# MLA latents and one chunk of the feed-forward input turned on VectorE in a two-layer decoder trunk

## The chip, the core and the metric

The kernel runs on one core of a Trainium2 chip. The metric is the time of one execution on the device, in microseconds (us). Engines are called by the profile's names: PE is TensorE, DVE is VectorE, ACT is ScalarE, POOL is GpSimd, and SP issues the loads. All arithmetic is float32.

## The reference, cut to what matters

```python
for l in range(DEPTH):                      # 2 layers, SEQ 256, D_MODEL 2048
    h = rmsnorm(x, g_mix[l])
    (fq, fk, fv, ff, cq, ckv, kr, uv, dq, dk, dv) = jnp.split(h @ w_in[l], pts, axis=-1)
    ...
    y_b = mla_mixer(cq, ckv, kr, g_cq[l], g_ckv[l], w_uq[l], w_ukv[l], cos_mla, sin_mla)
    ...
    x = x + jnp.concatenate([y_a, y_b, y_c, y_d], axis=-1) @ w_o[l]
    x = x + memory_cross_attention(rmsnorm(x, g_cross[l]), mem_n, ...)
    x = x + swiglu(rmsnorm(x, g_ffn[l]), w_gate[l], w_up[l], w_down[l])
return rmsnorm(x, g_final)

def mla_mixer(c_q, c_kv, k_rope, g_cq, g_ckv, w_uq, w_ukv, cos, sin):
    q = _heads(rmsnorm(c_q, g_cq) @ w_uq, MLA_HEADS)       # c_q: 256 x 384
    kv = _heads(rmsnorm(c_kv, g_ckv) @ w_ukv, MLA_HEADS)   # c_kv: 256 x 256
    ...
def swiglu(xn, w_gate, w_up, w_down):                      # hidden width 5632
    return (jax.nn.silu(xn @ w_gate) * (xn @ w_up)) @ w_down
```

## The kernel before

The 256 rows of x stand on the partitions as two tiles of 128, and the 2048 columns are four chunks of 512 (`self.x[c]`). Every large product is split in two float32r parts on either side: a weight block is copied to `whi` by ACT (line 204) and the rest `wlo = raw - whi` is made by DVE (line 210). Each product then takes three matmuls (lines 303 to 305): left high by `whi`, left high by `wlo`, left low by `whi`. The left operand must stand turned, with the contracted columns on the partitions, so a normalised chunk of x becomes `fT_hi` (ACT, line 206) and `fT_lo` (DVE, line 212) after a transpose. The row factor of the norm is applied later, to the product.

There are two ways to turn. `turn` (line 420) uses PE: 128x128 transposes against the identity into PSUM. `turn_blocks` (line 429) uses DVE: sixteen 32x32-block transposes for a chunk, into an SBUF tile `raw`, four to a step.

`drive` sets the order on all engines; it is written out as a program, and each engine runs its own part of it in order. Work is cut into groups (one product of 512 columns, such as `gate` of one hidden block), and groups into units of two k-tiles, which are 12 matmuls. For unit i the loop first converts the weights of unit i + 3 (`AHEAD` is 3), then issues the matmuls of unit i, then calls `step`, which advances every running task (a Python generator) by one `yield`. So what a task issues is placed between units, and a `yield` is one unit. If a unit needs a chunk whose task has not ended, `need` drains the task there, after the conversion of unit i + 3 and before the matmuls of unit i. `whi` and `wlo` have 5 buffers, so the conversion for unit i + 3 waits until PE is done with unit i - 2. SBUF tiles of one chunk's size come from a ring of 21 slots.

The latents: group `m1` gives cq (384 columns), `m2` gives ckv (256). `latent` squares, scales by the norm, and turns the two or three 128-column blocks on PE (tiles `cqtp`, `ckvtp`). In program order the turning of cq falls behind units 4 and 5 of `m2`, that of ckv behind unit 4 of `dk`; cq is used by `uqr` and `uqn` (after `dk`), ckv by `ukn` after them. Group `dq`, which came first, is being turned by DVE at the same time (tile `dqT`, two transposes a step), and `gates` makes the forget gate's cumulative sums.

The feed-forward input: `wco` (cross attention's output product) has four groups, one for each chunk c of x, of two units each. When group c ends, `into_x` adds it to x (line 950) and starts `norm_chunk`: squares first, and from the third step on, PE transposes (tile `xT`) with the high and low parts. The first `gate` product then takes the chunks in the order 0, 1, 2, 3, two units to a chunk. In two other places of a layer (`wo` into cT, `down` into hT) `norm_chunk` runs with `early`, that is with `turn_blocks`, for the first three chunks.

Of the kernel before, what the change touches and what calls it, by code (L numbers as in the profile page):

```python
# [25 lines left out]
NC = 4  # L26
# [115 lines left out]
class Kernel:  # L142
# [196 lines left out]
        stats = self.const.tile([P, T * NC], F32, name=name + "st")  # L339
        return Split(NC), stats[:].rearrange("p (t c) -> p t c", t=T)  # L340

    def norm_chunk(self, st, c, g, name, early):

        nc, xs, stats, xc = self.nc, st[0], st[1], self.x[c]
        part = xs.parts[c] = self.split_tile(name)
        for t in range(T):
            self.square_sum(xc[:, t, :], stats[:, t, c : c + 1])
        st[4] += 1
        yield
        yield  # L350
        if early:
            raw = self.slot("xT")
            yield from self.turn_blocks(xc[:], raw)
            yield
        for b in range(2):
            tv = raw[:, 2 * b : 2 * b + 2, :] if early else self.turn(xc, 2 * b, 2, "xT")
            self.split_turned(tv, part, 2 * b, self.gains[:, g, 4 * c + 2 * b : 4 * c + 2 * b + 2])
            yield
# [63 lines left out]

    def turn_blocks(self, nat, dst, n=4):

        src = nat.rearrange("p t (c b i) -> p t c b i", c=4, b=4)
        for i in range(16):
            a, b = i % 4, i // 4
            o = dst[32 * b : 32 * b + 32].rearrange("p c (t a j) -> p t c a j", t=T, a=4)
            self.nc.vector.transpose(o[:, :, :, a, :], src[32 * a : 32 * a + 32, :, :, b, :])  # L429
            if i % n == n - 1:  # L430
                yield
# [231 lines left out]
    def latent(self, nat, w, nk, off, l, name, xs):  # L663

        nc = self.nc
        ss = self.sm(name + "ss", T)
        for t in range(T):
            self.square_sum(nat[:, t, :], ss[:, t : t + 1])
        rc = self.rms(ss[:], T, w, name + "r")
        for _ in range(3):  # L670
            yield
        for t in range(T):
            nc.vector.tensor_scalar(nat[:, t, :], nat[:, t, :], rc[:, t : t + 1], None, ALU.mult)
        yield
        yield
        part = xs.parts[0]
        for b in range((nk + 1) // 2):
            n = min(2, nk - 2 * b)
            tv = self.turn(nat, 2 * b, n, name + "tp")
            self.split_turned(tv, part, 2 * b, self.gsm[:, l, off + 2 * b : off + 2 * b + n])  # L680
            yield

    def gates(self, z, rows, own):
# [258 lines left out]
        for c in range(NC):  # L942
            yield Group("wo", self.blocks("w_o", l, c), 512, y, False, self.into_x(c, st, 1 + 3 * l, "cT", c < NC - 1), O_ORDER, begin=mem if c == NC - 1 else None, hold=0 if c else 4)

    def into_x(self, c, st=None, g=None, name=None, early=False):

        def f(ps):
            for t in range(T):
                x = self.x[c][:, t, :]
                self.nc.vector.tensor_tensor(out=x, in0=ps[t][:], in1=x, op=ALU.add)  # L950
            if st is not None:
                st[0].tasks[c] = [self.soon(self.norm_chunk(st, c, g, name, early))]
                if c == NC - 1:
                    self.norm_after(st)
        return f
# [125 lines left out]
    def cross(self, l, norm, st, memT, mres):  # L1081
        s = {}
        y, cT = Split(1), norm[0]

        def out_q(ps):
            nat = self.slot("cq", shape=(P, T, 512))
            self.out_natural(ps, 0, 512, nat, self.times(norm[2][0], 128.0 ** -0.5))
            s["q"] = self.slot("cqT")
            yield
            yield from self.turn_blocks(nat[:], s["q"])  # L1090

        def done_q(ps):
            norm[3].drain()
            s["tq"] = self.soon(out_q(ps))

        def done_k(ps):
            self.mem_rms.drain()
            kT = self.slot("ckT")
            s["tk"] = self.soon(self.out_turned(ps, kT, mres[1]))
            s["p"] = [self.slot("cpT", shape=(P, 2, 512)) for _ in range(2)]  # L1100
            s["heads"] = [self.later(self.attend_memory((s["tq"], s["tk"]), s["q"], kT, h, s["p"][h // 2][:, h % 2, :])) for h in range(4)]

        def out_v(ps, hh):
            if hh == 0:
                s["v"] = self.slot("cv", shape=(P, T, 512))
                y.parts[0] = self.split_tile("yc")
            v = s["v"]
            self.out_natural(ps, 0, 256, v[:, :, 256 * hh : 256 * hh + 256], mres[0])
            yield
            for t in s["heads"][2 * hh : 2 * hh + 2]:  # L1110
                t.drain()
            o = self.bank("co")
            for i in range(2):
                h = 2 * hh + i
                for kt in range(2):
                    self.nc.tensor.matmul(o[:, i * S : (i + 1) * S], v[:, kt, h * P : (h + 1) * P], s["p"][hh][:, i, kt * S : (kt + 1) * S], start=(i == 0 and kt == 0), stop=(i == 1 and kt == 1))
            ov = o[:].rearrange("p (i s) -> p i s", i=2)
            self.split(ov, y.parts[0][0][:, 2 * hh : 2 * hh + 2, :], y.parts[0][1][:, 2 * hh : 2 * hh + 2, :])

        def done_v(hh):  # L1120
            def f(ps):
                s["tv%d" % hh] = self.soon(out_v(ps, hh))
                if hh == 1:
                    y.tasks[0] = [s["tv0"]]
                    y.late = s["tv1"]
            return f

        yield Group("cq", self.blocks("w_cq", l), 512, cT, False, done_q)
        yield Group("ck", self.blocks("w_ck", l), 512, memT, True, done_k)
        for hh in range(2):  # L1130
            yield Group("cv", self.blocks("w_cv", l, hh, 8), 256, memT, False, done_v(hh))
        for c in range(NC):
            yield Group("wco", self.blocks("w_co", l, c), 512, y, False, self.into_x(c, st, 2 + 3 * l, "fT"), hold=0 if c else 1)


    def ffn(self, l, norm, st):
        nc, a, fT = self.nc, self.a, norm[0]
        s = {}

        def done_gate(ps):  # L1140
            norm[3].drain()
            r = norm[2][0]
            s["g"] = self.slot("silu", shape=(P, T, 512))
            for t in range(T):
                nc.scalar.activation(s["g"][:, t, :], ps[t], AF.Silu, bias=0.0, scale=r[:, t : t + 1])

        def out_up(ps, g, part):
            r = norm[2][0]
            for t in range(T):
                nc.vector.scalar_tensor_tensor(out=g[:, t, :], in0=ps[t], scalar=r[:, t : t + 1], in1=g[:, t, :], op0=ALU.mult, op1=ALU.mult)  # L1150
            yield
            raw = self.slot("hidT")
            yield from self.turn_blocks(g, raw)
            for b in range(2):
                self.split(raw[:, 2 * b : 2 * b + 2, :], part[0][:, 2 * b : 2 * b + 2, :], part[1][:, 2 * b : 2 * b + 2, :])
                yield

        def done_up(hid, j):
            def f(ps):
                hid.parts[j] = self.split_tile("hid")  # L1160
                hid.tasks[j] = [self.soon(out_up(ps, s["g"], hid.parts[j]))]
            return f

        for j0, j1 in ((0, 6), (6, NCH)):
            hid = Split(j1 - j0)
            for j in range(j0, j1):
                yield Group("gate", self.blocks("w_gate", l, j), 512, fT, False, done_gate)
                yield Group("up", self.blocks("w_up", l, j), 512, fT, False, done_up(hid, j - j0))
            for c in range(NC):
                w = [(a["w_down"][l, c, b], 4) for b in range(j0, j1)]  # L1170
                if j1 < NCH:
                    done = self.into_x(c)
                elif l + 1 < L:
                    done = self.into_x(c, st, 3 * (l + 1), "hT", c < NC - 1)
                else:
                    done = self.final(c, st[1])
                yield Group("down", w, 512, hid, False, done, last=(l == L - 1 and j1 == NCH and c == NC - 1))
# [170 lines left out]
```

## Time and profile before

| | |
|---|---|
| median of 3 runs | 2336.83 us (2336.59 to 2338.02) |
| the profiled execution | 2337.07 us, of which the trace spans 2335.4 us |
| PE busy | 2322.1 us of the span |
| DVE busy | 1501.7 us |
| ACT busy | 1132.1 us |
| POOL busy | 231.1 us |
| mean granted PE clock | 0.999 of full speed |

Matmuls overlap, so the duration shown for one (390 ns for 512 columns) is longer than the time from one start to the next. What a stretch of PE costs is read from the starts. The times of a row are in us from the start of the span.

### The profile page before, as it was taken

How to read it: one execution, taken by the hardware profiler on the slowest of the kernel's cores; microseconds unless marked ns; L12 is line 12 of the kernel's file. 1: busy time of each engine (PE TensorE's matmuls, PEld its weight loads, DVE VectorE, ACT ScalarE, POOL GpSimd, SP SyncE). 2: the span in 40 equal slices, each digit the busy share in tenths (PEclk: the TensorE clock that was granted, in tenths of full speed). 3: DMA queues.
4: the chain of work that ended last, by engine and by line, in shares of the span. 5: the costliest groups of instructions: out<-in, count | busy, mean ns of one | idle time of the engine just before them, and what ended most of it. 6: DMA issues, size and time to landing. Idle time of an engine off the chain costs nothing.

```text
span 2335.4 us, 28342 instructions
## 1 busy us (share of the span) xinstructions
PE 2322.1 (99%) x10992; PEld 1950.9 (84%) x10992; DVE 1501.7 (64%) x2183; ACT 1132.1 (48%) x1611; POOL 231.1 (10%) x174
## 2 busy tenths in 40 slices
PE   9999999999999999999999999999999999999998
PEld 8888889888888888888898888898888888888886
DVE  6846796566766446767766567955666564476564
ACT  7656554644444344444455565636444433344443
POOL 1221340100000000000012314301000000000001
PEclk9999999999999999999999999999999999999999
DMA  8644565455555555555545454644555555555543
GB/s 295 223 165 164 190 214 183 165 196 181 195 202 198 195 187 188 193 204 186 194 165 193 163 175 166 215 180 162 211 183 186 213 190 191 197 180 199 216 180 126
DMA packets 69719, 444.24 MB, mean 190 GB/s; under 512 B 8000, under 2 KB 10064, under 8 KB 19920
## 3 DMA queue, kind: packets, MB, share of 16 engines
q1 hardware_dynamic: 67328, 435.52, 52.4%
q0 software_dynamic: 2112, 6.85, 0.9%
q8 instruction: 86, 1.41, 0.2%
q14 instruction: 49, 0.40, 0.1%
q10 hardware_dynamic: 144, 0.06, 0.0%
HBM read 440.30 MB, written 2.10 MB: 189 GB/s over the span
## 4 chain that ended last, share of the span: by engine, by line
PE 94%; DVE 2%; POOL 1%; issue 1%; ACT 1%; DMA 0%; SPq 0%; POOLq 0%; DVEq 0%; ACTq 0%
PE gate L304 7%; PE gate L303 7%; PE up L304 7%; PE gate L305 7%; PE up L305 7%; PE up L303 7%; PE down L305 7%; PE down L303 7%; PE down L304 7%; PE wo L303 2%; PE wo L305 2%; PE wo L304 2%; DVE wlo L210 1%; PE fv L303 1%; PE ck L317 1%
## 5 line engine op out<-in xcount | busy, mean ns | idle before, releaser
L210 DVE TENSOR_TENSOR wlo<-raw,whi 128x1024 fp32r<-128x1024 f32 (+3 forms) x772 | 932.2, 1221 | 548.6 <-ACT whi L204 542.0
L204 ACT CAST whi<-raw 128x1024 fp32r<-128x1024 f32 (+2 forms) x828 | 842.8, 1037 | 652.5 <-PE up L305 246.6
L303 PE MATMUL gate<-whi,fT_hi 128*128 128x512 f32 x704 | 274.7, 390 | 0.0
L305 PE MATMUL gate<-whi,fT_lo 128*128 128x512 f32 x704 | 274.0, 389 | 0.0
L304 PE MATMUL gate<-wlo,fT_hi 128*128 128x512 f32 x704 | 273.9, 389 | 0.0
L303 PE MATMUL up<-whi,fT_hi 128*128 128x512 f32 x704 | 273.9, 389 | 0.0
L304 PE MATMUL up<-wlo,fT_hi 128*128 128x512 f32 x704 | 273.9, 389 | 0.0
L305 PE MATMUL up<-whi,fT_lo 128*128 128x512 f32 x704 | 273.9, 389 | 0.0
L303 PE MATMUL down<-whi,hid_hi 128*128 128x512 f32 x704 | 273.9, 389 | 0.0
L304 PE MATMUL down<-wlo,hid_hi 128*128 128x512 f32 x704 | 273.9, 389 | 0.0
L305 PE MATMUL down<-whi,hid_lo 128*128 128x512 f32 x704 | 273.9, 389 | 0.0
L210 POOL TENSOR_TENSOR wlo<-raw,whi 128x1024 fp32r<-128x1024 f32 x56 | 144.9, 2592 | 389.4 <-ACT whi L204 389.4
L429 DVE STREAM_TRANSPOSE hidT<-silu 32x256 f32<-32x256 f32 x352 | 153.3, 436 | 5.7
L305 PEld LDWEIGHTS gate<-whi,fT_lo 128*128 128x128 f32 x704 | 132.1, 188 | 27.6
L303 PEld LDWEIGHTS up<-whi,fT_hi 128*128 128x128 f32 x704 | 132.1, 188 | 27.5
L305 PEld LDWEIGHTS down<-whi,hid_lo 128*128 128x128 f32 x704 | 132.1, 188 | 27.5
L304 PEld LDWEIGHTS down<-wlo,hid_hi 128*128 128x128 f32 x704 | 132.1, 188 | 27.5
L304 PEld LDWEIGHTS up<-wlo,fT_hi 128*128 128x128 f32 x704 | 132.1, 188 | 27.4
L305 PEld LDWEIGHTS up<-whi,fT_lo 128*128 128x128 f32 x704 | 132.1, 188 | 27.4
L303 PEld LDWEIGHTS down<-whi,hid_hi 128*128 128x128 f32 x704 | 132.1, 188 | 27.3
L303 PEld LDWEIGHTS gate<-whi,fT_hi 128*128 128x128 f32 x704 | 132.2, 188 | 27.3
L304 PEld LDWEIGHTS gate<-wlo,fT_hi 128*128 128x128 f32 x704 | 132.2, 188 | 27.2
(426 smaller groups left out, 3340.5 us busy)
## 6 DMA issues: line engine op xcount, KB each, us to landing
raw<-in_w_gate SPq DMA_DIRECT2D x88, 1024.0 KB, 4.8
raw<-in_w_up SPq DMA_DIRECT2D x88, 1024.0 KB, 4.8
raw<-in_w_down SPq DMA_DIRECT2D x88, 1024.0 KB, 4.8
raw<-in_w_o SPq DMA_DIRECT2D x32, 1024.0 KB, 4.8
raw<-in_w_dk SPq DMA_DIRECT2D x8, 1024.0 KB, 5.0
raw<-in_w_dv SPq DMA_DIRECT2D x8, 1024.0 KB, 6.8
raw<-in_w_fq SPq DMA_DIRECT2D x8, 1024.0 KB, 4.8
raw<-in_w_fk SPq DMA_DIRECT2D x8, 1024.0 KB, 4.9
```

The lines of the kernel that those rows point to most:

```text
L204: self.nc.scalar.copy(hi, src)
L210: (eng or self.nc.vector).tensor_tensor(out=lo, in0=src, in1=hi.bitcast(F32), op=ALU.subtract)
L303: mm(o, xh, wh, start=(i == 0), stop=False)
L304: mm(o, xh, wl, start=False, stop=False)
L305: mm(o, xl, wh, start=False, stop=(i == len(g.ks) - 1))
L317: mm(o, l, g.xs.hi(k), start=False, stop=end)
L429: self.nc.vector.transpose(o[:, :, :, a, :], src[32 * a : 32 * a + 32, :, :, b, :])
```

## The change

cq and ckv are turned by `turn_blocks` into a slot `raw` (32x192 and 32x128 per transpose), and the high and low parts are made one or two steps after the last quarter. Chunk 0 of the feed-forward input is turned by `turn_blocks` too, after five more steps of waiting (`rest`). The first `gate` group of a layer takes its k-tiles 4 to 15 first and 0 to 3 last.

```diff
-    def norm_chunk(self, st, c, g, name, early):
+    def norm_chunk(self, st, c, g, name, early, rest):
...
         if early:
+            for _ in range(rest):
+                yield
             raw = self.slot("xT")
             yield from self.turn_blocks(xc[:], raw)
             yield
...
-        src = nat.rearrange("p t (c b i) -> p t c b i", c=4, b=4)
+        src = nat.rearrange("p t (c b i) -> p t c b i", b=4, i=32)
...
         part = xs.parts[0]
+        raw = self.slot(name + "tp")
+        yield from self.turn_blocks(nat, raw[:, :nk, :])
+        yield
         for b in range((nk + 1) // 2):
             n = min(2, nk - 2 * b)
-            tv = self.turn(nat, 2 * b, n, name + "tp")
-            self.split_turned(tv, part, 2 * b, self.gsm[:, l, off + 2 * b : off + 2 * b + n])
+            self.split_turned(raw[:, 2 * b : 2 * b + n, :], part, 2 * b, self.gsm[:, l, off + 2 * b : off + 2 * b + n])
             yield
...
-    def into_x(self, c, st=None, g=None, name=None, early=False):
+    def into_x(self, c, st=None, g=None, name=None, early=False, rest=0):
...
-            yield Group("wco", self.blocks("w_co", l, c), 512, y, False, self.into_x(c, st, 2 + 3 * l, "fT"), hold=0 if c else 1)
+            yield Group("wco", self.blocks("w_co", l, c), 512, y, False, self.into_x(c, st, 2 + 3 * l, "fT", c == 0, 5), hold=0 if c else 1)
...
-                yield Group("gate", self.blocks("w_gate", l, j), 512, fT, False, done_gate)
+                blocks, ks = self.blocks("w_gate", l, j), None
+                if j == 0:
+                    blocks, ks = blocks[1:] + blocks[:1], list(range(4, 4 * NC)) + list(range(4))
+                yield Group("gate", blocks, 512, fT, False, done_gate, ks=ks)
```

## Rows read from the trace of the kernel before

**Rows 1.** The page: busy time by engine, and the chain that ended last.

```profile
PE 2322.1 (99%) x10992; PEld 1950.9 (84%) x10992; DVE 1501.7 (64%) x2183; ACT 1132.1 (48%) x1611; POOL 231.1 (10%) x174
...
PE 94%; DVE 2%; POOL 1%; issue 1%; ACT 1%; DMA 0%; SPq 0%; POOLq 0%; DVEq 0%; ACTq 0%
```

**Rows 2.** Waits of PE: who for whom, us in total, times, longest.

```profile
PE qrtp L420 <- POOL kr L571: 0.4, 2, 0.2
PE dk L304 <- DVE wlo L210: 0.2, 1, 0.2
```

**Rows 3.** Timeline of PE, layer 0, wco: start, duration, engine, line, what.

```profile
434.80 0.39 PE L303 MATMUL wco<-whi,yc_hi 128*128 128x512 f32 x1
...
437.52 0.60 PE L420 MATMUL xT<-ident,x 128*128 128x128 f32 x4
...
440.73 1.03 PE L420 MATMUL xT<-ident,x 128*128 128x128 f32 x8
...
444.38 0.60 PE L420 MATMUL xT<-ident,x 128*128 128x128 f32 x4
```

**Rows 4.** Timeline of PE, layer 1, units 4 to 7 of m2.

```profile
1216.07 0.60 PE L420 MATMUL cqtp<-ident,cq 128*128 128x128 f32 x4
...
1218.27 0.38 PE L420 MATMUL cqtp<-ident,cq 128*128 128x128 f32 x2
...
1220.25 0.31 PE L303 MATMUL m<-whi,hT_hi 128*128 128x320 f32 x1
...
1222.01 0.39 PE L303 MATMUL dk<-whi,hT_hi 128*128 128x512 f32 x1
```

**Rows 5.** Timeline of PE, layer 0, from m2's unit 5 into dk.

```profile
56.20 0.78 PE L420 MATMUL cqtp<-ident,cq 128*128 128x128 f32 x4
...
62.94 0.50 PE L304 MATMUL dk<-wlo,hT_hi 128*128 128x512 f32 x1 [0.22 <-DVE wlo L210]
...
72.14 0.39 PE L304 MATMUL dk<-wlo,hT_hi 128*128 128x512 f32 x1
```

**Rows 6.** Groups of DVE by form: busy us, mean ns of one.

```profile
L429 DVE STREAM_TRANSPOSE xT<-x 32x256 f32<-32x256 f32 x144 | 62.7, 436 | 2.3
```

**Rows 7.** Timeline of DVE, layer 0, around the turning of cq.

```profile
59.97 0.89 DVE L429 STREAM_TRANSPOSE dqT<-dq 32x256 f32<-32x256 f32 x2
60.88 0.88 DVE L212 SCALAR_TENSOR_TENSOR cqT_lo<-cqtp,gsm,cqT_hi 128x256 fp32r<-128x256 f32 x2
61.67 1.22 DVE L210 TENSOR_TENSOR wlo<-raw,whi 128x1024 fp32r<-128x1024 f32 x1
62.91 0.89 DVE L429 STREAM_TRANSPOSE dqT<-dq 32x256 f32<-32x256 f32 x2
63.83 0.48 DVE L212 SCALAR_TENSOR_TENSOR cqT_lo<-cqtp,gsm,cqT_hi 128x256 fp32r<-128x256 f32 x1
64.23 1.22 DVE L210 TENSOR_TENSOR wlo<-raw,whi 128x1024 fp32r<-128x1024 f32 x1
...
69.20 1.22 DVE L210 TENSOR_TENSOR wlo<-raw,whi 128x1024 fp32r<-128x1024 f32 x1
```

**Rows 8.** The tile dqT: durations min/median/max, first and last start.

```profile
L429 DVE STREAM_TRANSPOSE dqT<-dq x32: 426/436/442, 53.0 to 1213.9; 32x256 f32<-32x256 f32 x32
```

**Rows 9.** Timeline of DVE, a chunk turned in quarters behind wo, layer 0.

```profile
295.51 1.77 DVE L429 STREAM_TRANSPOSE xT<-x 32x256 f32<-32x256 f32 x4
297.31 1.64 DVE L210 TENSOR_TENSOR wlo<-raw,whi 128x1024 fp32r<-128x1024 f32 x1
```

**Rows 10.** Timeline of DVE, layer 0, around units 1 and 2 of the first gate group.

```profile
452.72 0.87 DVE L212 SCALAR_TENSOR_TENSOR fT_lo<-xT,gains,fT_hi 128x256 fp32r<-128x256 f32 x2
...
453.77 1.23 DVE L210 TENSOR_TENSOR wlo<-raw,whi 128x1024 fp32r<-128x1024 f32 x1
455.50 0.88 DVE L212 SCALAR_TENSOR_TENSOR fT_lo<-xT,gains,fT_hi 128x256 fp32r<-128x256 f32 x2 [0.50 <-ACT fT_hi L206]
```

**Rows 11.** Timeline of ACT, layer 0, the copy of uv.

```profile
101.35 1.08 ACT L411 COPY lv<-uv 128x512 f32<-128x512 f32 x2 [3.11 <-POOL kr L571]
```

More of the change, by code (lines that the diff above doesn't have):

```diff
@@ L951, in f @@
             if st is not None:
-                st[0].tasks[c] = [self.soon(self.norm_chunk(st, c, g, name, early))]
+                st[0].tasks[c] = [self.soon(self.norm_chunk(st, c, g, name, early, rest))]
                 if c == NC - 1:
```

## The prediction

> **What bounds the kernel now.** I read the page first. PE is busy for 2322 of 2335 us, and the chain that ended last is PE for 94% [rows 1]. DVE is busy for 1502 us, so on average it has a third of its time to spare. The view of PE's waits comes next: PE hardly waits for anyone, and what little there is has DVE's low parts and POOL's rotary key at its other end [rows 2]. So the time is the number of things that stand in PE's queue, and a transpose that leaves the queue gives back its slot. Then come the timelines of PE and DVE at the places that change, because the average says nothing about a stretch of 10 us: the question is whether DVE has room there.
>
> **What leaves PE.** I price a transpose from starts. In wco, 12 matmuls take 437.52 - 434.80 = 2.72 us [rows 3]. With four transposes ahead of them the distance is 440.73 - 437.52 = 3.21, with eight 444.38 - 440.73 = 3.65. So four cost 0.49 and eight 0.93, 0.12 each. Chunk 0's first four stand alone and its second four share the group of eight: 0.49 + 0.44 = 0.93 us per layer. In m2 a clean unit takes 1222.01 - 1220.25 = 1.76; the unit with four takes 2.20 and that with two 1.98 [rows 4], so cq's six cost 0.44 + 0.22. Ckv's four fall in dk, whose matmuls have wco's width: 0.48. The latents are 1.14 us per layer. All 36 transposes together are 2 x (0.93 + 1.14) = 4.1 us, which is 0.18% of the time, and about 0.4 us of waits could go with them [rows 2, 5]. That is the most that the change can bring.
>
> **What DVE gets.** A transpose of 32x256 takes 0.436 us [rows 6], a quarter of four 1.80 from start to the next instruction [rows 9]. Chunk 0 costs 7.2 us of DVE to save 0.93 of PE. The forms 32x192 and 32x128 don't occur before. Bounds: in proportion to the columns (0.33 and 0.22), and as long as 32x256 (0.44). I take a fixed part plus columns: low parts of 256 and 1024 columns take 0.48 and 1.22 [rows 7], so a column is about 1 ns, which leaves 0.19 fixed and gives 0.375 and 0.31. A quarter is then 1.5 us for cq (1.3 to 1.8) and 1.24 for ckv (0.9 to 1.8). The loop's order gives the places.
>
> The Trainium skill (VectorE: DVE Perf Modes, "Rules for kernel authors") speaks against this change: it advises TensorE for a 128x128 transpose where PSUM will do as the place of the result. Its section "The three transpose paths" gives 311 ns for VectorE and 390 for TensorE (bf16). The trace here has 0.12 us on PE [rows 3] and, for the same data, 7.0/8 = 0.87 us on DVE [rows 6]. By the page's VectorE figure, as an estimate, chunk 0 would take 2.5 us instead of 7.2 and the stall below would be gone.
>
> **Chunk 0 and the gate group.** Chunk 0's task starts behind wco's third unit. Two steps, five of `rest`, and the first quarter stands behind gate unit 1; the others stand behind units 2, 3, 4. The next step is empty, and gate unit 6, which uses chunk 0, drains the task: the high and low parts come there, behind the conversion for unit 6 + 3. So between the first quarter and the first low part DVE must also make the `wlo` of five units and chunk 3's low parts. In order: the `wlo` of gate unit 4 began at 453.77 [rows 10] and moves with PE to 452.84. From there four times `wlo` and a quarter, 4 x (1.24 + 1.80) [rows 7, 9]; chunk 3's two pairs of low parts, 2 x 0.79 [rows 7]; the `wlo` of two units of `up`, 2 x 1.2; chunk 0's first low part, 0.48. That ends at 452.84 + 12.16 + 1.58 + 2.4 + 0.48 = 469.5. PE: one clean unit from 437.52, six with four transposes (6 x 3.21), two clean ones: unit 6 begins at 464.9, and its third matmul, which reads the low part, would begin at 465.4. It waits 4.1 us. Overlap of neighbouring DVE instructions (0.09 between the first two kinds of [rows 7]) takes up to 1.3 off; waits for ACT like the 0.50 in [rows 10] put 0.5 on: 2.8 to 4.6. Queued behind the waiting matmul is all of PE, and nothing later gives this back. Net 4.1 - 0.93 = +3.2 a layer, +6.3 in both. The new order itself costs nothing: chunk 3 is asked for two units earlier, but its parts are ready some 5 us before unit 4.
>
> **cq in layer 0.** DVE works without a gap there and is already late: PE waits for dk's first `wlo` at 62.94 [rows 5]. The reason is dq's turning, two transposes in every step [rows 7]. Now four quarters of 1.5 join it behind m2's units 4 to 7, and the three low parts (60.88 to 61.67 and 63.83 to 64.23, 1.2 us) leave this stretch. So the `wlo` of dk's unit 3 moves from 69.20 to 69.20 + 6.0 - 1.2 = 74.0 and ends at 75.3. PE asked for it at 72.14 [rows 5]: it comes 3.15 us late, although it has lost six transposes by then. (Bounds 2.4 and 4.35, by the quarter.) Then dq's turning ends and DVE gets ahead again.
>
> **ckv in layer 0.** Its quarters stand behind dk's units 4 to 7: 1.24 + 1.24 per unit of 2.72, so DVE holds its place. But the low parts stand behind the conversion of uv, only one short unit ahead of ukn. Carried on from the state that cq leaves, the last quarter ends at 93.4, the `wlo` of ukn and uv at 95.8, the first low part at 96.2; PE asks at 95.4. I take 0.85 (0 to 3.1). Ckv's transposes give 0.48 back, and PE's wait for the rotary key [rows 2] goes, 0.2, as PE is later than POOL. Layer 0: 3.15 + 0.85 - 0.68 = +3.3 (1.7 to 7.0).
>
> **Layer 1.** Dq's last pair starts at 1213.9 [rows 8], before the turning of cq would begin (1216.07, [rows 4]), so the quarters have DVE's steps nearly for themselves: 1.24 + 1.5 for each, against PE's 1.76 in m2 and 2.72 in dk. The lead of three units holds; the narrowest place has 0.4 us left, and ckv has 0.6 at ukn. So -1.14 (up to +1.3 with the long quarter).
>
> Three slots more per layer are taken from the ring of 21. Where a slot comes free late, its next writer waits, as ACT's copy of uv does for 3.1 us [rows 11], of which PE sees 0.2 [rows 2]. I put this at nothing; the upper bounds have room for it.
>
> **Sum.** 6.3 + 3.3 - 1.1 = +8.5 us on 2337.07, the profiled execution's own time (its span is 2335.4). The median of the runs is 0.24 less: 2345.3.
>
> **Rivals.**
> - *All of it is hidden.* DVE keeps up, PE loses 36 transposes and the 0.4 us of waits: 2332.3, just short of 0.2% faster. For it: DVE's average. Against: it needs 4.1 us less work between two fixed places in the gate group. It decides from quarters of about 0.8 us on. Chance 0.08, half of it beyond the edge of 0.2%.
> - *The gate group is hidden, cq in layer 0 is not.* -1.9 + 3.3 - 1.1 = +0.3: 2337.1. This is what DVE transposes at the page's price would give. Chance 0.12.
> - *The latents are hidden, the gate group is not.* 6.3 - 1.5 - 1.1 = +3.7: 2340.5. It needs short quarters in both latents. Chance 0.08.
> - *The stall also costs PE its clock.* In gate unit 6 PE stands still twice, some 2.3 us for ACT's high part and, two matmuls later, 1.8 for the low one. Before, the clock granted is 0.999 on the mean. At 1.2 instead of 2.4 GHz a unit of 12 takes 2.72 us more [rows 3]; one unit at each of the two places makes +5.4: 2350.7. The Trainium skill (TensorE: Matmul & The Clock Gate, Part 1) has the engine fall to the lower clock after idling and come back only after activity; no row here shows the lower level. Chance 0.06.
>
> **How the numbers follow.** The case of the sum has 0.66. Its bounds: 2 x (2.8 - 0.93) + 1.7 - 1.1 = +4.3 and 2 x (4.6 - 0.93) + 7.0 + 1.3 = +15.6, so 2341.1 to 2352.4. A measurement here tells about 0.2%, or 4.7 us, from no change: below 2332.2 is faster, above 2341.5 slower. Slower: 0.66 + 0.06, less 0.02 for the low end. Same: 0.12 + 0.08 + 0.04 + 0.02. Faster: 0.04. A range of 2340 to 2352 holds the case of the sum, the clock and the hidden latents, 0.80.
>
> **What would show it.** PE has 10956 matmuls. PE's waits: in either layer 2 to 5 us for fT_hi and fT_lo in the first gate group; in layer 0 about 3 us for the `wlo` of dk, nothing in layer 1. DVE without a gap from gate unit 1 to unit 6. The timeline gives the two new forms' times. I am wrong if the first gate group shows no wait, that is if the quarters or the order of the drain are not as I read them.

## The result, and the profile after

The changed kernel takes 2357.94 us (median of 5 runs, 2354.36 to 2359.06) against 2336.85 (5 runs, 2336.59 to 2338.30) for the kernel before on the same chip. The ratio is 1.0086, 95% interval 1.0076 to 1.0097: slower, by 21 us at the median where 8.5 were forecast. The time lies above the range of 2340 to 2352.

The profiled execution is the shortest of the five: 2354.36 us, a span of 2352.6, 17.3 us above the profiled execution of before. Its mean granted PE clock is 0.998; the other four show 0.996 or 0.997. Before it was 0.999. The page of the changed kernel has, as [rows 1] has for before, busy time by engine and the chain that ended last:

```profile
PE 2323.9 (99%) x10956; PEld 1949.0 (83%) x10956; DVE 1536.7 (65%) x2279; ACT 1133.9 (48%) x1611; POOL 231.3 (10%) x174
...
PE 91%; DVE 4%; issue 1%; POOL 1%; ACT 1%; DMA 1%; SPq 0%; POOLq 0%; DVEq 0%; ACTq 0%
```

PE lost its 36 transposes and is busy 1.8 us longer all the same, although DVE still has a third of its time to spare: the stretches at the lower clock, below, are one reason (a matmul is longer there). PE's longest waits; of these places only dk's stood in the list before, with 0.2 us [rows 2]:

```profile
PE dv L303 <- ACT ukn L395: 4.3, 2, 2.5
PE gate L303 <- ACT fT_hi L206: 3.8, 2, 1.9
PE gate L305 <- DVE fT_lo L212: 3.0, 2, 1.5
PE dk L304 <- DVE wlo L210: 3.0, 3, 1.6
PE ukn L316 <- DVE ckvT_lo L212: 1.8, 2, 1.6
```

Four of these five lines were foreseen in the prediction. The first, the largest, was not. To price each place, I take the start of each group's first matmul, after minus before. How far that difference moves over a place is what the place cost. (The last start used is that of `up` in layer 1; behind it nothing moves.)

| place | predicted, us | measured, us |
|---|---|---|
| chunk 0's transposes, two layers | -1.87 | -0.94 and -0.93 |
| gate unit 6, two layers | +8.2 | +4.00 and +5.60 |
| layer 0, m2 and dk | +2.67 | +3.44 |
| layer 0, ukn | +0.85 | +1.83 |
| layer 0, PE at `dv` | 0 | +2.03 |
| layer 0, rotary key | -0.2 | -0.24 |
| layer 1, m2 and dk | -1.14 | -0.66 and -0.48 |
| layer 1, ukn | 0 | +1.18 |
| layer 1, PE at `dv` | 0 | +2.64 |
| layer 1, rotary key | 0 | -0.27 |
| sum | +8.5 | +17.2 |

The gate unit. PE's timeline of layer 1, start and duration, a bracket with the idle time and who ended it:

```profile
1638.42 0.50 PE L303 MATMUL gate<-whi,fT_hi 128*128 128x512 f32 x1 [1.90 <-ACT fT_hi L206]
1638.75 0.40 PE L304 MATMUL gate<-wlo,fT_hi 128*128 128x512 f32 x1
1640.66 0.50 PE L305 MATMUL gate<-whi,fT_lo 128*128 128x512 f32 x1 [1.51 <-DVE fT_lo L212]
...
1641.52 0.63 PE L305 MATMUL gate<-whi,fT_lo 128*128 128x512 f32 x1
1641.95 0.63 PE L303 MATMUL gate<-whi,fT_hi 128*128 128x512 f32 x1
...
1644.51 0.53 PE L303 MATMUL gate<-whi,fT_hi 128*128 128x512 f32 x1
1644.88 0.39 PE L304 MATMUL gate<-wlo,fT_hi 128*128 128x512 f32 x1
```

PE stands still twice, as forecast. From start to start the two gaps are together 3.7 us longer than two usual ones of 0.23 us. Behind them the matmuls from 1641.52 to 1644.88 start 0.43 us apart instead of 0.23: 1.2 instead of 2.4 GHz, for eight matmuls, which costs 1.55 us. In layer 0 the same two waits have no such stretch behind them in this execution, so that place cost 4.00. The view by windows shows it too; the number after POOL's busy time is the granted PE clock, in shares of full speed:

```profile
1620.00:1640.00 20.00, 17.24 (x81) 13.61 (x79) 18.30 (x33) 12.39 (x22) 1.61 (x1) 1.00 0.49 172
1640.00:1660.00 20.00, 19.34 (x78) 15.84 (x79) 9.22 (x12) 9.05 (x10) 0.00 (x0) 0.91 0.48 168
```

DVE in the same unit of layer 0, as [rows 9] and [rows 10] show it before:

```profile
470.34 1.23 DVE L210 TENSOR_TENSOR wlo<-raw,whi 128x1024 fp32r<-128x1024 f32 x1
471.59 1.80 DVE L431 STREAM_TRANSPOSE xT<-x 32x256 f32<-32x256 f32 x4
473.42 2.36 DVE L210 TENSOR_TENSOR wlo<-raw,whi 128x1024 fp32r<-128x1024 f32 x2
475.70 1.67 DVE L212 SCALAR_TENSOR_TENSOR fT_lo<-xT,gains,fT_hi 128x256 fp32r<-128x256 f32 x4
```

The last quarter, two `wlo`, then the low parts, without a gap: the order that the prediction read from the loop.

The wait at `dv` in layer 0, on PE, ACT and POOL:

```profile
105.62 0.50 PE L303 MATMUL dv<-whi,hT_hi 128*128 128x512 f32 x1 [1.86 <-ACT ukn L395]
```
```profile
97.92 1.09 ACT L395 ACTIVATE uqn<-uqn 128x512 f32<-128x512 f32 x2 [1.44 <-POOL kr L573]
...
104.48 1.09 ACT L395 ACTIVATE ukn<-ukn 128x512 f32<-128x512 f32 x2 [3.93 <-POOL kr L573]
...
107.01 1.08 ACT L413 COPY lv<-uv 128x512 f32<-128x512 f32 x2
```
```profile
102.05 1.72 POOL L572 TENSOR_TENSOR kr<-rope 128x256 f32<-128x256 f32 x1
103.73 0.72 POOL L573 TENSOR_TENSOR kr<-rope 128x256 f32<-128x256 f32 x1
```

ACT copies `ukn` out of PSUM into a slot of the ring, and that slot is free only when POOL's rotary step ends (103.73 + 0.72 = 104.45). The slot that is missing then seems to be ckv's (`e3_own_tile` below tests it): its low parts, the last to read it, end at 98.16 (97.17 + 0.99, below), behind the start of the copy of `uqn`; cq's low parts end at 80.67. Until the copy has emptied that bank (104.48 + 1.09 = 105.57), `dv` can't write, and it starts at 105.62. Before, it was ACT's copy of `uv`, one copy further on, that waited for POOL, 3.11 us [rows 11], and PE saw nothing of it.

DVE around the two latents of layer 0, as [rows 7] shows it before:

```profile
61.32 1.51 DVE L431 STREAM_TRANSPOSE cqtp<-cq 32x192 f32<-32x192 f32 x4
62.86 1.22 DVE L210 TENSOR_TENSOR wlo<-raw,whi 128x1024 fp32r<-128x1024 f32 x1
...
92.31 1.00 DVE L210 TENSOR_TENSOR wlo<-raw,whi 128x512 fp32r<-128x512 f32 x1
93.34 1.26 DVE L431 STREAM_TRANSPOSE ckvtp<-ckv 32x128 f32<-32x128 f32 x4
94.63 2.62 DVE L210 TENSOR_TENSOR wlo<-raw,whi 128x1024 fp32r<-128x1024 f32 x2
97.17 0.99 DVE L212 SCALAR_TENSOR_TENSOR ckvT_lo<-ckvtp,gsm,ckvT_hi 128x256 fp32r<-128x256 f32 x2
```

The two new forms take 1.51 and 1.26 us a quarter; the estimates were 1.5 and 1.24. What stands beside them is slower than elsewhere: the `wlo` of 512 columns takes 1.00 us where the shortest of its kind takes 0.69, the pair behind it 2.62 instead of the 2.36 in the gate group above, and the pair of low parts 0.99 instead of 0.88 [rows 7]. POOL is at its rotary steps from 91.05 to 104.45; that the two hold each other up here is not shown (`e5_gate_pool` below has such a case).

### The profile page after: what moved, and what is told of

Its sections match the earlier page's. It is cut to its first block, busy times and chain, and to the rows that moved or that the text cites. A ratio compares the mean times of both kernels' runs of the same rounds, so it can differ in the third digit from the quotient of the medians.

```text
span 2352.6 us, 28351 instructions
## 1 busy us (share of the span) xinstructions
PE 2323.9 (99%) x10956; PEld 1949.0 (83%) x10956; DVE 1536.7 (65%) x2279; ACT 1133.9 (48%) x1611; POOL 231.3 (10%) x174
## 4 chain that ended last, share of the span: by engine, by line
PE 91%; DVE 4%; issue 1%; POOL 1%; ACT 1%; DMA 1%; SPq 0%; POOLq 0%; DVEq 0%; ACTq 0%
PE up L305 7%; PE up L304 7%; PE up L303 7%; PE down L304 7%; PE down L303 7%; PE down L305 7%; PE gate L305 6%; PE gate L303 6%; PE gate L304 6%; PE wo L305 2%; PE wo L304 2%; PE wo L303 2%; DVE wlo L210 1%; PE fv L303 1%; PE ck L317 1%
```

## The experiments

Theory: the loss is three things. First, DVE's late parts (gate unit 6, dk and ukn of layer 0). Second, ckv's tile `raw`, which is still in use when `uqn` and `ukn` take their slots of the ring, so that these get slots that come free later. Third, PE's clock, which falls to 1.2 GHz behind some of the stops, in more places in the other executions than in the profiled one. Rivals: the two parts disturb each other; the ring has nothing to do with the wait at `dv`; the clock falls for a reason other than PE's stops; DVE is short of time over the whole stretch, not just at the end of chunk 0.

The kernel before took 2336.8 us beside the first four experiments, 2337.48 beside the next four, and 2337.21 beside the last three.

**Each part alone.** `e1_latents_only` is the change without the two edits at `wco` and `gate`; `e2_gate_only` is the change without the edit in `latent`.

> The latents are turned on DVE; the feed-forward part is as before the change. Theory (each part costs what its own place shows in the timeline of the changed kernel): layer 0 loses 3.4 us by dk's end, 1.8 at ukn and 2.0 where dv waits for ACT's copy of ukn, less 0.2 and 0.3; layer 1 wins 0.7 and 0.5 and loses 1.2 and 2.6, less 0.3. Together about +9.3 us, 2346.2, with a spread between runs as small as before (1 to 2 us), because the long waits of PE in the gate group are gone. Rival (the latents are near nothing and PE's clock makes the excess): within 2 us of the kernel before.

> Chunk 0 is turned on DVE and the gate order is 1, 2, 3, 0; the latents are turned on PE. Theory: in each layer PE wins 0.93 us and waits 3.7 at gate unit 6, so +5.6 us or 2342.4 at full clock; on top of that a stretch at half clock behind the wait in some executions, 1 to 5 us, so 2342 to 2348 and a spread of several us. Rival (the stalls add up only together with the latents'): +5.6 with no spread, or less.

Measured: 2349.9 us (2348.69 to 2350.93), ratio 1.0055 (1.0040 to 1.0070), and 2346.41 us (2346.24 to 2348.18), ratio 1.0043 (1.0026 to 1.0060). The losses are 13.1 and 9.6; their sum is 22.7, and the changed kernel's is 21.1. The 1.6 us between the two lie within the intervals, so no sign is left of the parts feeding each other, and each loses by itself. By the same table of starts, the gate part alone costs -0.93 +5.56 and -0.94 +5.57: what the changed kernel showed, with the stretch at 1.2 GHz in both layers. The latents alone show the steps of the table (+2.03 and +2.63 at `dv`) and a stretch that I had not expected, behind the wait at `dv`. PE there:

```profile
104.61 0.61 PE L303 MATMUL dv<-whi,hT_hi 128*128 128x512 f32 x1 [1.84 <-ACT ukn L395]
105.01 0.63 PE L304 MATMUL dv<-wlo,hT_hi 128*128 128x512 f32 x1
...
107.57 0.63 PE L304 MATMUL dv<-wlo,hT_hi 128*128 128x512 f32 x1
108.00 0.52 PE L305 MATMUL dv<-whi,hT_lo 128*128 128x512 f32 x1
108.36 0.39 PE L303 MATMUL dv<-whi,hT_hi 128*128 128x512 f32 x1
```

Again eight matmuls some 0.43 us apart, and the same recurs in layer 1. In the profiled execution of the whole change neither `dv` has it.

**The ring.** `e3_own_tile` is the changed kernel with ckv's `raw` outside the ring:

```diff
-        raw = self.slot(name + "tp")
+        raw = self.slot(name + "tp") if nk == 3 else self.turned.tile([P, 2, 256], F32, tag="turned", name=name + "tp")
```

> The changed kernel, with ckv's turned copy in a tile of its own instead of a slot of the ring. Theory (the third slot of the mixers, held until ukn, makes ACT's copies of uqn and ukn take slots that POOL still uses): the waits of dv for ACT's copy of ukn (2.0 and 2.6 us) and of uv for uqn's (0.3) go, 4.5 to 5 us less than the changed kernel. Rival (POOL is late for another reason, DVE's transposes hold it up): the waits stay, time as the changed kernel's.

Measured: 2352.18 us (2349.60 to 2353.59), ratio 1.0064 (1.0049 to 1.0079), 5.8 below the changed kernel. The wait at `dv` is gone from PE's list, and ACT's copy now follows PE alone:

```profile
102.31 1.09 ACT L396 ACTIVATE ukn<-ukn 128x512 f32<-128x512 f32 x2 [1.86 <-PE ukn L318]
...
105.92 1.08 ACT L414 COPY lv<-uv 128x512 f32<-128x512 f32 x2 [0.98 <-POOL kr L574]
```

POOL's wait is back at the copy of `uv`, where it was before the change, although cq's tile is still in the ring. So it is the ring, and ckv's slot in it. This profiled execution (2353.51 us) also shows longer stretches at 1.2 GHz in the gate group: ten matmuls in either layer, and the gate's places cost +6.23 and +6.34.

**Is DVE short only at the end?** `e4_rest0` starts chunk 0's quarters five units earlier (`rest` 0 instead of 5).

> The changed kernel without the five steps of rest ahead of chunk 0's quarters. Theory (the stall at gate unit 6 is work that stands in front of chunk 0's low part since the quarters start too late): the quarters lie behind wco's last four units and DVE has its lead back by gate unit 6, so no wait there: 2 x 3.7 us less than the changed kernel and no stretch at half clock, 2346 to 2348, with a small spread. Rival (DVE is short in the whole stretch, wherever the quarters stand): PE waits earlier instead, at wco's last units or at chunk 1's low parts, and the time stays above 2350.

Measured: 2351.03 us (2349.87 to 2352.23), ratio 1.0060 (1.0045 to 1.0075). The wait in unit 6 is gone, but another took its place. (The waits in dk, at ukn and at `dv` are about those of the changed kernel, the one at `dv` of layer 0 with a stretch at 1.2 GHz behind it.) The new line among PE's waits, and one of them on the timeline:

```profile
PE xT L422 <- DVE fT_lo L212: 3.9, 4, 1.7
```
```profile
463.56 0.63 PE L422 MATMUL xT<-ident,x 128*128 128x128 f32 x4 [1.69 <-DVE fT_lo L212]
```

The transposes of the other chunks stand on PE and wait for a PSUM bank, which DVE empties late. The gate's place still costs 2.3 us a layer instead of 4.0, so the rival is half right: wherever the quarters stand in this stretch, part of DVE's 7.2 us shows.

**Half of the `wlo` to POOL.** `e5_gate_pool` is the gate part with every second `wlo` of the first `gate` and `up` groups on POOL.

```diff
-POOLED = ("wco", "wo", "fk", "fv")
+POOLED = ("wco", "wo", "fk", "fv", "gate0", "up0")
```

> Only the gate part of the change (latents on PE), and every second wlo of the first gate and up group is made by POOL. Theory (gate unit 6 waits since DVE has 3.7 us too much to do ahead of chunk 0's first low part): three wlo of 1.24 us between the first quarter and that low part leave DVE, 3.7 us, so the wait shrinks to 0 to 0.5 and with it the stretch at half clock; what stays is the transposes' 0.93 a layer: 2335 to 2336, a small spread. Rival (the wait comes from the place of the parts in the order, not from DVE's load): the wait stays near 3.7 and the time near 2346.

Measured: 2343.0 us (2341.03 to 2344.34), ratio 1.0022 (1.0013 to 1.0031). A miss: PE still waits 4.1 us in all for `fT_hi` (3.8 in `e2_gate_only`), though only 0.8 instead of 3.0 for `fT_lo`, and the gate's place costs +3.00 and +3.02. DVE, and POOL at the same time:

```profile
459.30 1.79 DVE L431 STREAM_TRANSPOSE xT<-x 32x256 f32<-32x256 f32 x4
461.12 3.12 DVE L210 TENSOR_TENSOR wlo<-raw,whi 128x1024 fp32r<-128x1024 f32 x1
464.27 1.79 DVE L431 STREAM_TRANSPOSE xT<-x 32x256 f32<-32x256 f32 x4
```
```profile
458.38 4.78 POOL L210 TENSOR_TENSOR wlo<-raw,whi 128x1024 fp32r<-128x1024 f32 x2 [2.91 <-ACT whi L204]
```

DVE's `wlo` begins while POOL is busy (until 463.16) and takes 3.12 us instead of 1.22; the quarter of transposes beside POOL takes its usual 1.79. The 1.90 us that this one `wlo` took longer are nearly the 2.0 that PE then waits for `fT_hi` in this layer: much of what POOL took off DVE was lost again there. The Trainium skill (SBUF — State Buffer, "SBUF: two separate sides") says that a VectorE instruction with two inputs in SBUF and a GpSimd instruction that reads SBUF exclude each other: the one that starts first holds the other up for its whole length. The trace agrees: the `wlo`, with two inputs, ends 1.08 us behind POOL's, little less than the 1.22 that it takes alone, and the transposes, with one, were not held up.

**The clock.** `e6_filler` is the gate part with 16 matmuls, whose result nothing reads, between units 5 and 6 of the first gate group.

```diff
+            if u.group.name == "gate0" and u.i == 12:
+                junk = self.bank("junkps")
+                for _ in range(16):
+                    self.nc.tensor.matmul(junk[:], u.group.xs.hi(8)[:, :P], u.hi[:, :512], start=True, stop=True)
```

> Only the gate part of the change, and 16 matmuls (3.6 us) into an unused bank ahead of gate unit 6, where PE would wait. Theory (the stretch at half clock comes from PE standing still): PE is busy through the wait, so the 1.5 us per layer at half clock and the spread go, and the wait itself is filled: 2342 to 2343. Rival (half clock comes from something else, such as the load of DVE): 2346 as without the matmuls, with half clock still behind unit 6. Second rival (the wait is not where it seems): the 16 matmuls come on top, 2350 or more.

Measured: 2344.2 us (2343.3 to 2346.38), ratio 1.0031 (1.0019 to 1.0043), with a clock of 0.999 in every run. PE does the same useful work at the same pace as with the wait, since the filler takes the wait's place: the gate's place costs +3.97 and +4.01. But the stretch at 1.2 GHz is gone from both layers, and the loss fell from 9.6 to 6.7 us. The view by windows around gate unit 6, two lines of `e6_filler` and two of `e2_gate_only`, with the granted clock behind POOL's busy time:

```profile
464.00:476.00 12.00, 11.94 (x53) 9.54 (x52) 9.16 (x15) 3.70 (x6) 0.00 (x0) 1.00 0.50 177
1627.00:1640.00 13.00, 12.93 (x58) 10.36 (x57) 9.23 (x15) 4.21 (x7) 0.00 (x0) 1.00 0.44 161
```
```profile
464.00:476.00 12.00, 8.59 (x31) 6.31 (x30) 7.22 (x12) 2.64 (x5) 0.00 (x0) 0.86 0.50 175
1628.00:1640.00 12.00, 8.59 (x30) 6.30 (x29) 6.83 (x11) 3.04 (x6) 0.00 (x0) 0.86 0.48 175
```

DVE is no less busy than without the matmuls (9.16 and 9.23 us against 7.22 and 6.83 in these windows), so the stretch comes from PE's standing still; it costs about 1.6 us at each place. (The profiled execution of `e6_filler` took 2346.13 us; 3.0 us of that lie away from the gate, ahead of dk in layer 0 and between fq and ck in layer 1. So the reading rests on the gate's places, not on that one total.)

**cq alone.** `e8_cq_only` turns cq on DVE in both layers and leaves ckv and chunk 0 on PE. `e7_pool_cq1` is `e5_gate_pool` with cq on DVE in layer 1.

> Only cq turned on DVE, in both layers; ckv on PE, the gate part as before the change. Theory (cq costs in layer 0 alone, since dq is turned there at the same time; ckv's slot makes the waits at dv): +2.9 us by the end of dk in layer 0, no wait at ukn, at uv or dv, -0.66 in layer 1: about +2, 2338.5 to 2340. Rival (any slot more shifts the ring and makes ACT wait): 2 and 2.6 us more at dv, 2343 or more.

> The kernel with every second wlo of the first gate and up group on POOL, and also cq turned on DVE in layer 1 alone, where the changed kernel showed no wait for it (0.66 us won up to dk). Theory: 2 x 0.93 + 0.66 = 2.5 us less than the kernel before, 2334.3 to 2335. Rival (one slot more in layer 1 is enough to make ACT wait for POOL's slot, or POOL's wlo are late): 2336 or more.

Measured: `e8_cq_only` 2341.66 us (2340.95 to 2342.64), ratio 1.0017 (1.0008 to 1.0026). No wait at `ukn` or `dv`, so cq's slot alone doesn't disturb the copies, as in `e3_own_tile`. (A kernel with ckv's slot alone was not run.) The miss is in dk of layer 0, +5.70 instead of the changed kernel's +3.59. Most of the difference is ckv's transposes: they are back on PE (0.48) and wait there for DVE, which is still late with ckv's scaling:

```profile
PE ckvtp L420 <- DVE ckv L673: 1.2, 1, 1.2
```

`e7_pool_cq1`: 2342.67 us (2340.47 to 2345.09), ratio 1.0022 (1.0013 to 1.0031). It inherits the miss of `e5_gate_pool`, and of the 0.66 that m2 gives in layer 1, dk takes 0.29 back.

**Closing the account.** If the theory is right, other work for PE in front of unit 6 removes both the wait and the clock's part. `e9_hold` is the gate part with the first gate group's last two units, chunk 0's, placed behind the first two units of `up`, which takes its chunks in the same order:

```diff
-                yield Group("gate", blocks, 512, fT, False, done_gate, ks=ks)
-                yield Group("up", self.blocks("w_up", l, j), 512, fT, False, done_up(hid, j - j0))
+                yield Group("gate", blocks, 512, fT, False, done_gate, ks=ks, hold=0 if j else 6)
+                blocks = self.blocks("w_up", l, j)
+                if j == 0:
+                    blocks = blocks[1:] + blocks[:1]
+                yield Group("up", blocks, 512, fT, False, done_up(hid, j - j0), ks=ks)
```

`e10_hold_l1` adds cq and ckv on DVE in layer 1 alone, with ckv in its own tile. `e11_hold_all` is the whole change with the two units held and with ckv in its own tile.

> The gate part alone, with the first gate group's last two units (chunk 0's) placed behind the first two units of up, and up's chunks in the same order 1, 2, 3, 0. PE gets 24 matmuls or 5.4 us of other work at the place where it stood still for 3.7 us. If the gate part's loss is only the late low and high parts of chunk 0 and what the standing still does to the clock, no wait for fT_hi or fT_lo and no stretch at 1.2 GHz stay, and the transposes' 0.93 us a layer are all that is left: 1.9 us below the kernel before. If DVE's transposes cost PE something else in that stretch, such as later wlo in the groups behind it, the time stays at or above the kernel before.

> The kernel with chunk 0's units held, and in layer 1 alone cq and ckv turned on DVE, ckv's blocks in a tile of their own instead of a slot of the ring. By the account of the changed kernel, layer 1 gave 0.66 and 0.48 us at dk and uqr and lost its time only at ukn (0.4 to 0.6 us, late low parts) and at dv (slots of the ring, gone here): 0.5 to 1.1 us below the kernel with chunk 0's units held alone, 2.4 to 3.0 us below the kernel before. If the half clock comes without a wait too, or the ring is short by cq's slot as well, it is at or above the other kernel.

> The whole change in both layers, with chunk 0's units held behind up's first two and ckv's blocks in a tile of their own. What stays is the late DVE of layer 0: about 3.6 us at uqr, 1.8 at ukn, less 0.8 at m2 and 0.4 at the rotary product, so 4.2 us; in layer 1 about -0.5, in the gate groups -1.9. Sum 1.8 us above the kernel before, with little spread from run to run. If the three named costs (late parts in the gate group, ring, half clock behind waits) don't hold all of the loss, it stays 5 us or more above.

| | median, us | range | ratio, 95% |
|---|---|---|---|
| `e9_hold` | 2335.55 | 2334.59 to 2336.97 | 0.9991 (0.9982 to 1.0000) |
| `e10_hold_l1` | 2334.76 | 2334.03 to 2336.06 | 0.9989 (0.9981 to 0.9998) |
| `e11_hold_all` | 2338.93 | 2338.54 to 2339.99 | 1.0007 (0.9998 to 1.0016) |

Against 2337.21 these are -1.7, -2.4 and +1.7, where -1.9, -2.4 to -3.0 and +1.8 were expected. In `e9_hold` PE's waits no longer name `fT_hi` or `fT_lo`, and the transition from `up` to chunk 0's units has no bracket left (layer 0):

```profile
469.81 0.39 PE L303 MATMUL up<-whi,fT_hi 128*128 128x512 f32 x1
...
470.49 0.39 PE L303 MATMUL gate<-whi,fT_hi 128*128 128x512 f32 x1
...
470.94 0.39 PE L305 MATMUL gate<-whi,fT_lo 128*128 128x512 f32 x1
```

`e11_hold_all` still waits as in the changed kernel where nothing was done about it, in dk and ukn:

```profile
PE dk L305 <- DVE wlo L211: 3.0, 3, 1.6
PE ukn L317 <- DVE ckvT_lo L213: 1.8, 2, 1.6
```

With the two stops of the gate group and the two at `dv` out of the way, 19.4 of the 21.1 us are gone, the runs of `e11_hold_all` spread over 1.5 us instead of 4.7, and the clock is back at 0.999. `e10_hold_l1` is the fastest kernel here, 0.1% faster than before, with an interval that just stays below 1. The intervals of the other two hold 1, so by the times alone they are not told from no change, nor `e10_hold_l1` from `e9_hold`; what tells them apart is the places (in `e9_hold` -0.94 and -0.96 at the transposes and nothing lost at the gate).

## Why the prediction was right in direction and wrong in size

- *What leaves PE.* Right: 0.94 and 0.93 for chunk 0, 0.66 and 0.48 for the latents of layer 1, to the hundredth.
- *What DVE gets.* Right: 1.51 and 1.26 us a quarter. A 128x128 block of float32 costs 0.87 us on DVE here, so the rival built on shorter transposes (the gate hidden) is out.
- *Chunk 0 and the gate group.* Right in mechanism and size: gaps 3.7 us longer than usual where 4.1 were forecast.
- *cq in layer 0.* Right in mechanism, 0.8 too low: PE waits 3.0 us for DVE's late `wlo` (3.15 forecast), in three waits from dk's first unit on, not in one at unit 3. Beside them the sum had no term for PE's `cum` matmul, which waits 0.4 us for DVE's `lf` in the same stretch, nor for the 0.1 us that the first matmul behind a wait takes longer to the next start. The net at uqr is 3.44 instead of 2.67.
- *ckv in layer 0.* Too low: 1.83 at ukn, above the 0.85 taken, inside the bound of 3.1. The last quarter ended at 94.6 instead of 93.4, as all of dk ran later, and what follows it took some 0.3 us longer than the sum had it, at a time when POOL was busy. Layer 1, put at nothing, has the same place at 1.18. Part of that is the ring, since with ckv's own tile (`e3_own_tile`) it is 0.61.
- *The ring.* This is the first step that failed: "Three slots more per layer are taken from the ring of 21 ... I put this at nothing; the upper bounds have room for it." It cost 2.03 and 2.64 us. The row that mattered was in hand, ACT's copy of `uv` waiting 3.1 us for POOL [rows 11]. What I didn't ask is which copy would wait if one more slot were in use at that time: `ukn`, whose bank is the one that `dv` needs next. With both slots in the ring the wait is there (the changed kernel, `e1_latents_only`); with cq's alone it is not (`e3_own_tile`, `e8_cq_only`).
- *The clock.* The second failure: it stood as a rival with 0.06 and came true. 1.6 us of it lie in the profiled execution. I had asked for its chance in the gate group alone, at two places, and with a price of 2.72 us; there were four places, and a stretch cost some 1.6 at most of them. That a fall depends on PE's standing still is shown by `e6_filler`. That the 3.6 us between the profiled execution and the median are more such stretches is argued, not shown: the runs' mean clock (0.996 to 0.997 against 0.998) goes with it, `e1_latents_only` and `e2_gate_only` show stretches at places where the profiled execution had none, and in `e3_own_tile` the two gate places alone cost 3.0 us more than in it.

In the prediction's own sum: 8.5 forecast, +4.7 for the ring at `dv`, +1.6 for the clock, +2.2 for ukn in both layers, +0.8 for dk, and -0.5 for the gate's waits and the rotary key, makes 17.3, which is the profiled execution's 17.2 within rounding.

## What to carry to other kernels

Moving 0.12 us of PE work to an engine that needs 0.87 us for it pays only where that engine has the time in that very stretch and the result is wanted late enough; placing the consumer two units later was worth more than the move itself. A slot taken from a ring isn't free when the ring has room: a later writer may get one that comes free later, so look up who waits for a slot already and what stands behind the writer next to it. Where PE would stop, count the clock's fall behind the stop as part of the price, and work in the gap as the remedy.

## What the runs showed of the hardware that I had not expected

- Stops of PE of 1.8 us once (`dv`), or of 1.9 and 1.5 us with two matmuls between them (gate), were followed in some executions by six to ten matmuls of 512 columns at 1.2 GHz (starts 0.43 us apart), at a cost of 1.4 to 2.3 us, and in others not. No run shows what decides. In the changed kernel's profiled execution dq's matmuls are 0.43 us apart as well from 6.51 to 9.49, with no such stop ahead of them. That cost next to nothing: PE waits for DVE behind them anyway, and the first matmul of m1 starts 0.11 us later than before.
- A `wlo` on DVE took 3.12 us instead of 1.22 beside one on POOL, while DVE's transposes kept their 1.79.
